# Dilated attention stage: paired loads and broadcasts merged, the combination's small operations moved to GpSimd, output-weight splits moved later

## The chip, the core and the metric

The kernel runs on one core of a Trainium2 chip. A core has a TensorE (PE in the profile) that multiplies matrices out of SBUF into PSUM banks, a VectorE (DVE), a ScalarE (ACT), a GpSimd (POOL) and a SyncE (SP), and 16 DMA engines that move data between DRAM and SBUF. The metric is the device time of one execution in microseconds, as the median of several runs. The time before is 1261.68 us (three runs, 1260.31 to 1263.06).

## The reference

One layer of an encoder over 1024 tokens of width 1024, in float32. A normed input is projected into two mixers. The first is a latent attention of 8 heads (MLA). The second, on which the change works, is a mixture of three dilated attentions: 24 heads of 64 columns in three groups of 8, group g with window and dilation (128, 1), (512, 4), (2048, 16). The three groups are joined for each head slot with weights from their softmax denominators.

```python
def dilated_group(q, k, v, dilation, side):
    ...
    s = jnp.where(valid, s, NEG_INF)
    m = jnp.max(s, axis=-1, keepdims=True)
    p = jnp.exp(s - m)
    den = jnp.sum(p, axis=-1)
    o = jnp.einsum('brhnqk,brhnkd->brhnqd', p.astype(v.dtype), vb).astype(jnp.float32) / den[..., None]
    lse = m[..., 0] + jnp.log(den)
    ...

def dilated_mixture(q, k, v, positions):
    ...
    for g, (window, dilation) in enumerate(DIL_CONFIGS):
        ...
        o, lse = dilated_group(q[:, :, sl], k[:, :, sl], v[:, :, sl], dilation, window // (2 * dilation))
        ...
    alpha = jax.nn.softmax(jnp.stack(lses, axis=0), axis=0)
    out = jnp.sum(alpha[..., None] * outs, axis=0)
    ...

def hybrid_layer(...):
    ...
    y_mla = (a_out * jax.nn.silu(z_mla)) @ w_o_mla
    y_dil = (d_out * jax.nn.silu(z_dil)) @ w_o_dil
    merged = sigmoid(g_mla + b) * y_mla + sigmoid(g_dil + b) * y_dil
    return x + merged @ w_out
```

The last lines are shortened: both branches are gated, projected, summed, and go through w_out; a last norm follows.

## The kernel before

**Numbers.** Matrix products in float32 are made of three products of a high and a low part (`mm3`, L142). `split` (L148) makes the parts: ScalarE casts the high one (L150), another engine subtracts for the low one (L151). Tensors for TensorE are kept as float32r; in DRAM many lie as pairs of high and low, which is the index p with two values.

**Stages.** Up to 541 us the kernel projects the input: latents, tables, values, then queries, keys and part of the gates, which it stores to DRAM. From 541 to about 840 us it runs the dilated stage, to about 1133 us the MLA attention with the output projections of both branches fed between its steps, and then the product with w_out (`output`). From the dilated stage on the order of all instructions is written by hand; nothing is rescheduled.

**The dilated stage.** `plan` (L1281) lists four pairs of heads with five items each: the two heads of group 0, the two of group 1 (`dil_head`, four units each) and one item for both heads of group 2 (`dil_classes`, two units). That makes 20 items and 72 units. `attention` (L1296) runs over the units: at step t it issues the transposes of unit t, the scores of unit t + 2, and so on, with projection matmuls fed between (`feed`). When the last unit of an item has been issued up to its scores, the query and key loads (`load_qk`) of the item two further on are issued, and two steps after the last unit its value load (`load_v`).

**Loads.** All DMAs are issued from SyncE by one line (L140), one after another, in the order of the code; a DMA whose semaphore isn't there yet holds all behind it. The buffers are rings of places in SBUF: queries (`op_b`, shown as at_2048), keys (`op_a`, shown as at_1152 or at_1024) and values (`op_c`) have two places each. A query tile of `dil_head` has 128 partitions with 2 x 1024 values: partitions 0 to 63 hold the 64 columns of the head in high and low part, and partitions 64 to 127 hold the same again, so it is loaded in two DMAs of 64 rows from the same source. The key tile has the high part in partitions 0 to 63 and the low part in 64 to 127, again two DMAs. `dil_classes` makes four loads of queries and four of keys, each of 64 rows, beside memsets of the zero parts.

**The combination.** After the last unit of a pair, `combine` (L1351) joins the three groups in steps that are put at fixed numbers of units later: statistics are transposed and stored to DRAM (s_sd), read back with 16 rows of 64 tokens each (`by_token`), weights are formed on VectorE with operations on 16x128 (`differences`, L1386 to 1390; `factors`, L1398 and 1401; `quotients`, L1405 to 1408), and are stored as six rows of 1024 (s_rr). `spread` (L1411) loads each row into 64 partitions, half a row at a time, 12 DMAs of 128 KB a pair, into the ring `bc` of five places. `weighted` (L1418) multiplies the three numerators by these on VectorE (L1421) and adds them on GpSimd (L1423), and the last sum is stored (s_da) except for the last pair. The first spreads are issued at step 5, the first products at step 7. For the last pair the steps lie in the MLA attention, by `LAST_STEPS` (L35).

**The w_out splits.** w_out is loaded in half-rows of 128x512 into `bc`, from step 112 of the MLA attention on (`wout_load`), and each is split two steps later (L1045): the cast on ScalarE, the subtraction on GpSimd. The last of the first eight is split in `output` (L1458), before `mla_sum`, `mla_weighted` and `mla_merged`.

The lines that the prediction's steps turn on:

```python
            for rows in (slice(0, 64), slice(64, 128)):
                self.dma(q[rows], self.dq[g][h].rearrange("c r p t -> (c r) p t"))
            for p in range(2):
                self.dma(k[64 * p:64 * p + 64, :S + pad], self.dk[g][h].rearrange("c r p t -> p (c r) t")[p])
...
                for h in range(2):
                    self.dma(r[64 * h:64 * h + 64], self.rr[pair, 2 * g + h, c].partition_broadcast(64))
```

Of the kernel before, what the change touches and what calls it, by code (L numbers as in the profile page):

```python
# [33 lines left out]
LAST_JOBS = [(dt, 0) for dt in range(4)] + [(dt + i, half) for dt in (4, 6) for half in range(2) for i in range(2)] + [(dt, 1) for dt in range(4)]  # L34
LAST_STEPS = {2: 4, 3: 6, 4: 8, 5: 10, 7: 14, 8: 16, 9: 18}  # L35
PIECES = (1, 0, 0), (3, 0, 1), (14, 3, 0), (16, 3, 1), (18, 1, 0), (20, 1, 1), (24, 2, 0), (26, 2, 1)
# [24 lines left out]
class Net:  # L61
# [455 lines left out]
    def block_steps(self, n, item, ps, tp):  # L517
# [45 lines left out]
        parts = 2 if g < 2 else 1  # L563
        dst = (self.dq if which == 0 else self.dk)[g][4 * quad:4 * quad + 4]
        off = 64 if (g == 0 and which) else 0
# [52 lines left out]
        def store(half):  # L618
            for i in range(2):
                for j in range(4):  # L620
                    x = slice(32 * j, 32 * j + 32)
                    if g < 2:
                        self.dma(dst[j, i, :, :, off + 512 * half:off + 512 * half + 512], st[i, half][x])
                    elif half:
                        self.dma(dst[j, i, :, 0], st[i, 0][x])

# [361 lines left out]
    def mla_attention(self, later, first):  # L988
# [29 lines left out]
        for t in range(128):  # L1018
# [41 lines left out]
    def dil_head(self, pair, g, hh, st, nums):  # L1060
# [116 lines left out]
    def dil_classes(self, pair, st, nums):  # L1177
# [6 lines left out]
        def load_qk():  # L1184
            q = o["q"] = self.get("op_b", [128, 2, 8, 2, 64])
            k = o["k"] = self.get("op_a", [128, 2, 8, 64])
            for hh in range(2):
                h = 2 * pair + hh
                for e in range(2):
                    r, c = slice(64 * e, 64 * e + 64), slice(512 * e, 512 * e + 512)  # L1190
                    nc.gpsimd.memset(q[r, hh, :, 1 - e], 0.0)
                    self.dma(q[r, hh, :, e], self.dq[2][h].rearrange("c r p t -> (c r) (p t)")[:, c].rearrange("r (b m) -> r b m", b=8))
                    self.dma(k[r, hh], self.dk[2][h].rearrange("c r p t -> (c r) (p t)")[:, c].rearrange("r (b m) -> r b m", b=8))

# [156 lines left out]
    def combine(self, pair, st, nums):  # L1351

        nc = self.nc
        v = nc.vector
# [29 lines left out]
        def differences():  # L1384
            w = o["w"] = self.get("c_w", [16, 4, 2, 64])
            v.tensor_copy(w[:, 3], nat(0, 0))  # L1386
            for g in (1, 2):
                v.tensor_tensor(out=wv(3, g), in0=wv(3, g), in1=nat(0, g), op=ALU.min)
            for g in range(3):
                v.tensor_tensor(out=wv(g, g), in0=wv(3, g), in1=nat(0, g), op=ALU.subtract)  # L1390

# [3 lines left out]
        def factors():  # L1395
            d = nat(1, 0)
            for g in range(3):
                v.tensor_tensor(out=nat(1, g), in0=wv(g, g), in1=nat(1, g), op=ALU.mult)  # L1398
            for g in (1, 2):
                y = d.rearrange("p h (m c) -> p h m c", c=DIL[g])  # L1400
                v.tensor_tensor(out=y, in0=y, in1=nat(1, g), op=ALU.add)

        def quotients():
            w, d = o["w"], nat(1, 0)
            v.tensor_scalar(out=d, in0=d, scalar1=2.0, scalar2=None, op0=ALU.mult)  # L1405
            v.reciprocal(out=d, in_=d)
            for g in range(3):
                v.tensor_tensor(out=w[:, g], in0=w[:, g], in1=d, op=ALU.mult)
            self.dma(self.rr[pair].rearrange("y (x t) -> x y t", t=64), w[:, 0:3].rearrange("p g h t -> p (g h) t"))

        def spread(half, gs):  # L1411
            c = slice(512 * half, 512 * half + 512)
            for g in gs:
                r = o[g, half] = self.get("bc")
                for h in range(2):
                    self.dma(r[64 * h:64 * h + 64], self.rr[pair, 2 * g + h, c].partition_broadcast(64))

        def weighted(half, gs):  # L1418
            c = slice(512 * half, 512 * half + 512)
            for g in gs:  # L1420
                v.tensor_tensor(out=nums[g][:, c], in0=nums[g][:, c], in1=o[g, half], op=ALU.mult)  # L1421
                if g:
                    nc.gpsimd.tensor_tensor(out=nums[0][:, c], in0=nums[0][:, c], in1=nums[g][:, c], op=ALU.add)  # L1423
            if half and 2 in gs and pair < 3:
                self.dma(self.da[pair], nums[0])
        return {-1: statistics, 0: by_token, 2: differences, 3: lambda: (exponents(), factors()), 4: quotients,
                5: lambda: (spread(0, range(3)), spread(1, (0, 1))),
                7: lambda: (weighted(0, (0, 1)), spread(1, (2,))), 8: lambda: (weighted(0, (2,)), weighted(1, (0,))), 9: lambda: weighted(1, (1, 2))}


    def output(self):
# [25 lines left out]
        self.mla_copied(31)  # L1457
        self.wout_split(0, nc.gpsimd)  # L1458
        self.mla_sum(31)
        self.mla_weighted(31)  # L1460
        self.mla_merged(31, v)
        for i in range(3):
            self.wout_load(i, 1)
        self.one_bank = False
        ready = []
        for n in range(16):
            while self.jobs_done <= 16 + n:
                next(self.fill)
            if n % 2 == 0:
                self.wout_split(1, nc.gpsimd)  # L1470
                if n < 10:
# [51 lines left out]
    def run(self):  # L1523
        tc, nc = self.tc, self.nc
        with ExitStack() as ctx:
# [5 lines left out]

            self.dq = [dt(f"s_dq{g}", (8, 2, 32, 2 if g < 2 else 1, S), F32R if g < 2 else F32) for g in range(3)]
            self.dk = [dt(f"s_dk{g}", (8, 2, 32, 2 if g < 2 else 1, S + (128 if g == 0 else 0)), F32R if g < 2 else F32) for g in range(3)]
            self.dv = [dt("s_dv0", (S + 128, 1024), F32R), dt("s_dv1", (S, 1024), F32R), dt("s_dv2", (S, 512))]
# [158 lines left out]
```

## Time and profile before

| quantity | value |
|---|---|
| time, median of three runs | 1261.68 us (1260.31 to 1263.06) |
| time of the profiled execution | 1265.36 us |
| its span, first to last instruction | 1263.5 us |
| mean granted TensorE clock | 0.992 |
| moved by DMA over the span | 212.99 MB in 131602 packets, 169 GB/s in the mean |
| DMA engines busy, mean | 58.1% of 16 engines' span |

The slices of the span (40 of 31.6 us; a digit is the busy share in tenths, PEclk the granted clock in tenths):

```profile
PE   8989999999999999999989899999899999989997
DVE  7483524567567652345575776748777767659442
ACT  6533437344434345456554555636665655654232
POOL 2352217887777777445363230411420111157222
PEclk9989999999999999999999999999999999999999
DMA  9947675266556643497878797856543254234241
```

The dilated stage lies in slices 18 to 26. The DMA row is at 7 to 9 tenths through most of them, the highest for so long a stretch. VectorE is at 5 to 7 there, ScalarE at about 5, GpSimd at 2 to 6. Engines run beside each other, so a busy share says nothing by itself of what ends last; the waits of TensorE do.

### The profile page before, as it was taken

To read this page: it belongs to the slowest core of one execution; us is meant where nothing else is said; L and a number is where in the kernel's file an instruction comes from. 1 tells how busy PE (TensorE), PEld (TensorE's weight loads), DVE (VectorE), ACT (ScalarE), POOL (GpSimd) and SP (SyncE) were. 2 spreads that over 40 slices of the span, in tenths; PEclk is the share of its full clock that TensorE was granted. 3 is DMA by queue.
4 is the path that set the end of the run, shared out by engine and by line. 5 is a ranking of instruction groups with operands and counts; after the bars stand their busy time and mean duration, and the time that the engine had idled before them with its cause. 6 is when DMAs were issued, how large, how long until landed. Compare 5 with 4: busy or idle time off the path is not lost.

```text
span 1263.5 us, 19551 instructions
## 1 busy us (share of the span) xinstructions
PE 1214.5 (96%) x6909; PEld 1063.2 (84%) x6909; DVE 764.2 (60%) x1373; ACT 621.0 (49%) x1300; POOL 535.5 (42%) x433
## 2 busy tenths in 40 slices
PE   8989999999999999999989899999899999989997
PEld 7979999788888888888878787978788888878886
DVE  7483524567567652345575776748777767659442
ACT  6533437344434345456554555636665655654232
POOL 2352217887777777445363230411420111157222
PEclk9989999999999999999999999999999999999999
DMA  9947675266556643497878797856543254234241
GB/s 325 274 152 264 224 283 159 84 177 167 138 135 158 169 125 117 129 260 205 207 207 211 186 259 191 240 156 165 154 140 105 81 126 125 93 101 167 84 150 50
DMA packets 131602, 212.99 MB, mean 169 GB/s; under 512 B 36841, under 2 KB 67121, under 8 KB 127601
## 3 DMA queue, kind: packets, MB, share of 16 engines
q1 hardware_dynamic: 131504, 211.75, 58.1%
q8 instruction: 54, 0.88, 0.3%
q14 instruction: 44, 0.35, 0.1%
HBM read 145.05 MB, written 66.65 MB: 168 GB/s over the span
## 4 chain that ended last, share of the span: by engine, by line
PE 72%; DMA 9%; DVE 8%; ACT 4%; issue 3%; POOL 2%; SPq 1%; ACTq 0%; DVEq 0%; POOLq 0%
PE bank L144 6%; PE bank L146 5%; PE bank L145 5%; PE bank L852 3%; PE st_a L144 2%; PE st_a L145 2%; PE st_a L146 2%; PE st_d L145 2%; PE st_c L145 2%; PE st_c L146 2%; PE st_d L146 2%; PE st_d L144 2%; PE st_c L144 2%; PE pj L144 2%; PE pj L145 2%
## 5 line engine op out<-in xcount | busy, mean ns | idle before, releaser
L151 POOL TENSOR_TENSOR w_l<-w_raw,w_h 128x512 fp32r<-128x512 f32 x188 | 246.7, 1326 | 300.1 <-ACT w_h L150 252.5
L150 ACT CAST w_h<-w_raw 128x512 fp32r<-128x512 f32 x188 | 112.4, 620 | 103.7 <-POOL w_raw L495 95.1
L144 PE MATMUL bank<-at_r,w_h 128*128 128x512 f32 x344 | 141.9, 412 | 5.6 <-DVE at_f L792 3.0
L860 DVE TENSOR_TENSOR at_r<-bank,at_r 128x512 fp32r<-128x512 f32 x128 | 87.9, 688 | 79.8 <-ACT at_r L854 79.5
L146 PE MATMUL bank<-at_r,w_l 128*128 128x512 f32 x344 | 135.3, 393 | 0.0
L145 PE MATMUL bank<-at_r,w_h 128*128 128x512 f32 x344 | 135.1, 393 | 0.0
L854 ACT CAST at_r<-bank 128x512 fp32r<-128x512 f32 x128 | 74.9, 585 | 81.0 <-PE bank L852 80.1
L144 PE MATMUL pj<-w_h,at_r 128*128 128x256 f32 x384 | 109.7, 286 | 0.0
L145 PE MATMUL pj<-w_l,at_r 128*128 128x256 f32 x384 | 109.4, 285 | 0.0
L146 PE MATMUL pj<-w_h,at_r 128*128 128x256 f32 x384 | 109.4, 285 | 0.0
L1116 ACT ACTIVATE at_f<-at_f,at_f 128x256 f32<-128x256 f32 x128 | 64.1, 501 | 70.8 <-DVE at_f L1109 70.7
L495 POOL TENSOR_TENSOR w_raw<-w_raw 128x512 f32<-128x512 f32 x64 | 83.7, 1308 | 0.0
L1135 DVE TENSOR_TENSOR at_r<-bank,at_r 128x512 fp32r<-128x512 f32 x64 | 44.0, 687 | 63.7 <-ACT at_r L1131 63.4
L852 PE MATMUL bank<-consts,at_f 128*128 128x128 f32 x512 | 77.0, 272 | 3.1 <-DVE at_r L860 2.0
L144 PEld LDWEIGHTS bank<-at_r,w_h 128*128 128x128 f32 x344 | 65.2, 190 | 16.8 <-DVE at_f L792 4.2
L146 PEld LDWEIGHTS bank<-at_r,w_l 128*128 128x128 f32 x344 | 64.8, 188 | 14.6
L144 PEld LDWEIGHTS pj<-w_h,at_r 128*128 128x128 f32 x384 | 74.2, 193 | 0.9
L145 PEld LDWEIGHTS pj<-w_l,at_r 128*128 128x128 f32 x384 | 74.1, 193 | 0.8
L146 PEld LDWEIGHTS pj<-w_h,at_r 128*128 128x128 f32 x384 | 74.1, 193 | 0.7
L145 PEld LDWEIGHTS bank<-at_r,w_h 128*128 128x128 f32 x344 | 65.3, 190 | 8.7
L876 PE MATMUL bank<-at_r,at_r 128*128 128x256 f32 x256 | 67.6, 285 | 1.9 <-ACT at_r L854 1.8
L877 PE MATMUL bank<-at_r,at_r 128*128 128x256 f32 x256 | 67.4, 285 | 1.8 <-DVE at_r L860 1.8
(320 smaller groups left out, 3331.1 us busy)
## 6 DMA issues: line engine op xcount, KB each, us to landing
w_raw<-wt SPq DMA_DIRECT2D x48, 512.0 KB, 4.4
at_r<-s_dq SPq DMA_DIRECT2D x32, 512.0 KB, 7.0
s_dq<-dq_st SPq DMA_DIRECT2D x80, 128.0 KB, 2.4
s_dk<-dq_st SPq DMA_DIRECT2D x80, 128.0 KB, 2.4
s_dv<-dv_st SPq DMA_DIRECT2D x32, 256.0 KB, 3.0
zt<-s_gt SPq DMA_DIRECT2D x32, 256.0 KB, 3.5
w_raw<-wv SPq DMA_DIRECT2D x12, 512.0 KB, 4.8
at_f<-s_rr SPq DMA_DIRECT2D x48, 128.0 KB, 3.2
```

The source lines that it names most:

```text
L144: mm(out, lh, rh, start=start, stop=False, skip_group_check=skip)
L145: mm(out, lh, rl, start=False, stop=False, skip_group_check=skip)
L146: return mm(out, ll, rh, start=False, stop=stop, skip_group_check=skip)
L150: self.nc.scalar.copy(out=h, in_=raw)
L151: sub.tensor_tensor(out=l, in0=raw, in1=h.bitcast(F32), op=ALU.subtract)
L495: self.nc.gpsimd.tensor_tensor(out=b[out], in0=b[x], in1=b[y], op=ALU.subtract)
L852: self.nc.tensor.transpose(pt[:, o:o + 128], self.P[k, b][:, 128 * kc:128 * kc + 128], self.ident)
L854: self.nc.scalar.copy(out=h, in_=pt)
L860: self.nc.vector.tensor_tensor(out=l, in0=pt, in1=h.bitcast(F32), op=ALU.subtract)
L876: mm(out, vv[:, kc], ph[:, x], start=kc == 0, stop=False)
L877: mm(out, vv[:, kc], pl[:, x], start=False, stop=kc == 7)
L1116: nc.scalar.activation(out=p, in_=p, func=AF.Exp, scale=-1.0, bias=nm, accum_out=den)
```

## The change

It has four parts.

1. **Merged transfers.** In `dil_head` the two query loads become one of 128 rows whose source is the same 64 rows twice (a leading dimension of 2 with stride 0), and the two key loads one of 128 rows whose source begins with the part p. In `spread` the two DMAs of 64 partitions become one of 128 rows from two rows of s_rr, each repeated 64 times (source 2 x 64 x length), and groups 0 and 1 are fetched for both halves at once, into two places of `bc` side by side. Instead of 12 spreads a pair there are four. In `dil_classes` queries come in two DMAs of 64x16x64 and keys in one of 128x1024; for that s_dq2 and s_dk2 lie in DRAM in another order, and the stores to them are cut as 32x2x512.
2. **Small operations.** 11 of the 16x128 operations of each pair go from VectorE to GpSimd, the doubling before the reciprocal becomes an addition of the tile to itself there, and a copy is dropped.
3. **Products.** Of the six products of numerators with spreads, the two of group 1 go to GpSimd, and the products and sums are put in another order over steps 7 to 10.
4. **w_out splits.** They start at step 116 in place of 114, and the last ones of the first half follow `mla_merged`; the first load of the second half is issued at step 127.

```diff
-LAST_STEPS = {2: 4, 3: 6, 4: 8, 5: 10, 7: 14, 8: 16, 9: 18}
+LAST_STEPS = {2: 4, 3: 6, 4: 8, 5: 10, 7: 13, 8: 15, 9: 17, 10: 19}
...
-                        self.dma(dst[j, i, :, 0], st[i, 0][x])
+                        self.dma(dst[2 * quad + j // 2, :, i, :, j % 2].rearrange("e r t -> r e t"), st[i, 0][x].rearrange("r (e t) -> r e t", e=2))
...
-            if t >= 114 and t % 2 == 0:
+            if t >= 116 and t % 2 == 0:
                 self.wout_split(0, nc.gpsimd)
+            if t == 127:
+                self.wout_load(0, 1)
...
-            for rows in (slice(0, 64), slice(64, 128)):
-                self.dma(q[rows], self.dq[g][h].rearrange("c r p t -> (c r) p t"))
-            for p in range(2):
-                self.dma(k[64 * p:64 * p + 64, :S + pad], self.dk[g][h].rearrange("c r p t -> p (c r) t")[p])
+            src = self.dq[g][h:h + 1].rearrange("h c r p t -> h (c r) (p t)")
+            self.dma(q.rearrange("p a t -> p (a t)"), src.to_broadcast([2, 64, 2 * S]))
+            self.dma(k[:, :S + pad], self.dk[g][h].rearrange("c r p t -> p (c r) t"))
...
+            for e in range(2):
+                r = slice(64 * e, 64 * e + 64)
+                nc.gpsimd.memset(q[r, :, :, 1 - e], 0.0)
+                self.dma(q[r, :, :, e].rearrange("r h b m -> r (h b) m"), self.dq[2][pair, e].rearrange("c r h (b m) -> (c r) (h b) m", m=64))
+            self.dma(k.rearrange("p h b m -> p (h b m)"), self.dk[2][pair].rearrange("e c r h t -> (e c r) (h t)"))
...
-            v.tensor_copy(w[:, 3], nat(0, 0))
...
-                v.tensor_tensor(out=wv(g, g), in0=wv(3, g), in1=nat(0, g), op=ALU.subtract)
+                p.tensor_tensor(out=wv(g, g), in0=wv(3, g), in1=nat(0, g), op=ALU.subtract)
...
-                v.tensor_tensor(out=nat(1, g), in0=wv(g, g), in1=nat(1, g), op=ALU.mult)
+                p.tensor_tensor(out=nat(1, g), in0=wv(g, g), in1=nat(1, g), op=ALU.mult)
...
-                v.tensor_tensor(out=y, in0=y, in1=nat(1, g), op=ALU.add)
+                p.tensor_tensor(out=y, in0=y, in1=nat(1, g), op=ALU.add)
+            p.tensor_tensor(out=d, in0=d, in1=d, op=ALU.add)
...
-            v.tensor_scalar(out=d, in0=d, scalar1=2.0, scalar2=None, op0=ALU.mult)
             v.reciprocal(out=d, in_=d)
...
-                v.tensor_tensor(out=w[:, g], in0=w[:, g], in1=d, op=ALU.mult)
+                p.tensor_tensor(out=w[:, g], in0=w[:, g], in1=d, op=ALU.mult)
...
+        def spread(g, first, c):
+            r = o[g, c.start] = self.shaped(self.places["bc"][0] + first, [128, c.stop - c.start])
+            src = self.rr[pair, 2 * g:2 * g + 2, c].rearrange("h (a t) -> h a t", a=1)
+            self.dma(r, src.to_broadcast([2, 64, c.stop - c.start]))
...
+        def spreads():
+            spread(1, 0, both)
+            spread(0, 4096, both)
+            spread(2, 8192, halves[0])
...
+        def step8():
+            weighted(0, 0, v)
+            add(1, 0)
+            weighted(2, 0, v)
+            add(2, 0)
...
+        def step9():
+            spread(2, 2048, halves[1])
+            weighted(0, 1, v)
+            add(1, 1)
...
+                5: spreads, 7: lambda: (weighted(1, 0, p), weighted(1, 1, p)), 8: step8, 9: step9, 10: step10}
...
-        self.wout_split(0, nc.gpsimd)
         self.mla_sum(31)
         self.mla_weighted(31)
         self.mla_merged(31, v)
-        for i in range(3):
+        self.wout_split(0, nc.gpsimd)
+        for i in range(1, 3):
```

TensorE executes the same instructions in the same order before and after. What moves stands on the other engines. In the rows below a name with at_ is a place in SBUF with its size in values (at_2048 a query tile, at_1152 a key or value tile, at_512 and at_1024 spreads, statistics or numerators), a name with s_ a tensor in DRAM, and xN the count of equal instructions in a row.

SyncE's queue, in the second pair of heads, from the store of the weights (s_rr) of the first pair to the store of its result (s_da). Before:

```order
L140 DMA s_rr<-at_512_f 16x6x64
L140 DMA at_512_f<-s_rr 64x512 x10
L140 DMA s_zs<-zt 128x512
L140 DMA at_1152_r<-s_dv_69 128x8x128
L140 DMA at_512_f<-s_rr 64x512 x2
L140 DMA at_2048_f<-s_dq_64 64x8x64
L140 DMA at_1024_f<-s_dk_67 64x512
L140 DMA at_2048_f<-s_dq_64 64x8x64
L140 DMA at_1024_f<-s_dk_67 64x512
```

And after, at the same place:

```order
L140 DMA s_rr<-at_512_f 16x6x64
L140 DMA at_1024_f<-s_rr 128x1x1024 x2
L140 DMA at_512_f<-s_rr 128x1x512
L140 DMA s_zs<-zt 128x512
L140 DMA at_1152_r<-s_dv_69 128x8x128
L140 DMA at_2048_f<-s_dq_64 64x16x64 x2
L140 DMA at_1024_f<-s_dk_67 128x1024
L140 DMA s_zs<-zt 128x512
L140 DMA at_512_f<-s_rr 128x1x512
L140 DMA w_raw<-wt 128x1024
L140 DMA s_da<-at_1024_f 128x1024
```

Twelve spreads have become four, of which the last stands behind the class loads, and eight class loads have become three; the store of s_da still ends the row, and the next pair's first loads stand behind it.

The same queue a little earlier in that pair, as one piece of the difference, with the loads of a head of group 1:

```order
 L140 DMA s_zs<-zt 128x512
 L140 DMA at_1152_r<-s_dv_69 128x8x128
-L140 DMA at_2048_r<-s_dq_63 64x2048 x2
-L140 DMA at_1152_r<-s_dk_66 64x1024 x2
+L140 DMA at_2048_r<-s_dq_63 128x1x2048
+L140 DMA at_1152_r<-s_dk_66 128x1x1024
 L140 DMA w_raw<-wt 128x1024
 L140 DMA s_rr<-at_512_f 16x6x64
```

Each of the two pairs of 64-row loads has become one of 128 rows, at the same place of the queue.

GpSimd's queue after, at the first combination; zt are gate values, w_l low parts of projection weights, at_768 the statistics by token. In the queue of before the gate operations and the subtractions w_l stand there alone:

```order
L1390 TENSOR_TENSOR at_512_f<-at_512_f,at_768_f 16x128 x3
L1398 TENSOR_TENSOR at_768_f<-at_512_f,at_768_f 16x128
L1398 TENSOR_TENSOR at_768_f<-at_512_f,at_768_f 16x2x16x4
L1398 TENSOR_TENSOR at_768_f<-at_512_f,at_768_f 16x2x4x16
L1401 TENSOR_TENSOR at_768_f<-at_768_f 16x128 x2
L1402 TENSOR_TENSOR at_768_f<-at_768_f 16x128
L1408 TENSOR_TENSOR at_512_f<-at_512_f,at_768_f 16x128 x3
L722 TENSOR_TENSOR zt<-zt 128x512
L723 TENSOR_TENSOR zt<-zt 128x512
L151 TENSOR_TENSOR w_l<-w_raw,w_h 128x512 x2
L1424 TENSOR_TENSOR at_1024_f<-at_1024_f 128x512 x2
```

Twelve small operations (the first seven rows) now stand ahead of the gate operations and of the products of group 1 (the last row).

More of the change, by code (lines that the diff above doesn't have):

```diff
@@ L563, in block_steps @@
         parts = 2 if g < 2 else 1
-        dst = (self.dq if which == 0 else self.dk)[g][4 * quad:4 * quad + 4]
+        dst = (self.dq if which == 0 else self.dk)[g]
+        dst = dst[4 * quad:4 * quad + 4] if g < 2 else dst
         off = 64 if (g == 0 and which) else 0
@@ L1186, in load_qk @@
             k = o["k"] = self.get("op_a", [128, 2, 8, 64])
[L1187 to L1193, printed above, removed]
+            for e in range(2):
[3 more added lines that the diff above has]
+            self.dma(k.rearrange("p h b m -> p (h b m)"), self.dk[2][pair].rearrange("e c r h t -> (e c r) (h t)"))
         def load_v():
@@ L1353, in combine @@
         nc = self.nc
-        v = nc.vector
+        v, p = nc.vector, nc.gpsimd
+        both, *halves = slice(0, S), slice(0, 512), slice(512, S)
         o = {}
@@ L1385, in differences @@
             w = o["w"] = self.get("c_w", [16, 4, 2, 64])
-            v.tensor_copy(w[:, 3], nat(0, 0))
-            for g in (1, 2):
-                v.tensor_tensor(out=wv(3, g), in0=wv(3, g), in1=nat(0, g), op=ALU.min)
+            v.tensor_tensor(out=wv(3, 1), in0=nat(0, 0).rearrange("p h (m c) -> p h m c", c=DIL[1]), in1=nat(0, 1), op=ALU.min)
+            v.tensor_tensor(out=wv(3, 2), in0=wv(3, 2), in1=nat(0, 2), op=ALU.min)
             for g in range(3):
-                v.tensor_tensor(out=wv(g, g), in0=wv(3, g), in1=nat(0, g), op=ALU.subtract)
+                p.tensor_tensor(out=wv(g, g), in0=wv(3, g), in1=nat(0, g), op=ALU.subtract)
         def exponents():
@@ L1403, in quotients @@
         def quotients():
             w, d = o["w"], nat(1, 0)
-            v.tensor_scalar(out=d, in0=d, scalar1=2.0, scalar2=None, op0=ALU.mult)
             v.reciprocal(out=d, in_=d)
             for g in range(3):
-                v.tensor_tensor(out=w[:, g], in0=w[:, g], in1=d, op=ALU.mult)
+                p.tensor_tensor(out=w[:, g], in0=w[:, g], in1=d, op=ALU.mult)
             self.dma(self.rr[pair].rearrange("y (x t) -> x y t", t=64), w[:, 0:3].rearrange("p g h t -> p (g h) t"))
[L1411 to L1424, printed above, removed]
+        def spread(g, first, c):
+            r = o[g, c.start] = self.shaped(self.places["bc"][0] + first, [128, c.stop - c.start])
+            src = self.rr[pair, 2 * g:2 * g + 2, c].rearrange("h (a t) -> h a t", a=1)
+            self.dma(r, src.to_broadcast([2, 64, c.stop - c.start]))
@@ new lines, in spreads, with weighted, add @@
+        def spreads():
+            spread(1, 0, both)
+            spread(0, 4096, both)
+            spread(2, 8192, halves[0])
+        def weighted(g, half, eng):
+            c = halves[half]
+            x = o[g, c.start] if g == 2 else o[g, 0][:, c]
+            eng.tensor_tensor(out=nums[g][:, c], in0=nums[g][:, c], in1=x, op=ALU.mult)
+        def add(g, half):
+            c = halves[half]
+            p.tensor_tensor(out=nums[0][:, c], in0=nums[0][:, c], in1=nums[g][:, c], op=ALU.add)
@@ L1425, in weighted, with step10 @@
+        def step8():
[3 more added lines that the diff above has]
+            add(2, 0)
+            self.turn["bc"] = 4
+        def step9():
+            spread(2, 2048, halves[1])
+            weighted(0, 1, v)
+            add(1, 1)
+        def step10():
+            weighted(2, 1, v)
+            add(2, 1)
+            if pair < 3:
                 self.dma(self.da[pair], nums[0])
         return {-1: statistics, 0: by_token, 2: differences, 3: lambda: (exponents(), factors()), 4: quotients,
-                5: lambda: (spread(0, range(3)), spread(1, (0, 1))),
@@ L1428, in combine @@
-                7: lambda: (weighted(0, (0, 1)), spread(1, (2,))), 8: lambda: (weighted(0, (2,)), weighted(1, (0,))), 9: lambda: weighted(1, (1, 2))}
+                5: spreads, 7: lambda: (weighted(1, 0, p), weighted(1, 1, p)), 8: step8, 9: step9, 10: step10}
     def output(self):
@@ L1468, in output @@
                 next(self.fill)
-            if n % 2 == 0:
-                self.wout_split(1, nc.gpsimd)
-                if n < 10:
+            if n % 2 == 0 or n == 1:
+                self.wout_split(n > 0, nc.gpsimd)
+                if n % 2 == 0 and n < 10:
                     self.wout_load(n // 2 + 3, 1)
@@ L1530, in run @@
             self.mv = dt("s_mv", (S, 1024), F32R)
-            self.dq = [dt(f"s_dq{g}", (8, 2, 32, 2 if g < 2 else 1, S), F32R if g < 2 else F32) for g in range(3)]
-            self.dk = [dt(f"s_dk{g}", (8, 2, 32, 2 if g < 2 else 1, S + (128 if g == 0 else 0)), F32R if g < 2 else F32) for g in range(3)]
+            by_class = (4, 2, 2, 32, 2, 512)
+            self.dq = [dt(f"s_dq{g}", (8, 2, 32, 2, S), F32R) for g in range(2)] + [dt("s_dq2", by_class)]
+            self.dk = [dt(f"s_dk{g}", (8, 2, 32, 2, S + (128 if g == 0 else 0)), F32R) for g in range(2)] + [dt("s_dk2", by_class)]
             self.dv = [dt("s_dv0", (S + 128, 1024), F32R), dt("s_dv1", (S, 1024), F32R), dt("s_dv2", (S, 512))]
```

## The prediction, made before the changed kernel ran

> **What bounds the kernel now.** I read the busy table and the slices first, then the stretch in which the change lies by windows and waits, then its transfers.
>
> ```profile
> PE 1214.5 (96%) x6909; PEld 1063.2 (84%) x6909; DVE 764.2 (60%) x1373; ACT 621.0 (49%) x1300; POOL 535.5 (42%) x433
> 600.00:620.00 20.00, 20.00 (x132) 18.03 (x130) 12.40 (x33) 11.90 (x33) 8.14 (x7) 1.00 0.81 208
> 660.00:680.00 20.00, 16.20 (x104) 14.26 (x105) 12.16 (x28) 9.99 (x25) 8.50 (x8) 1.00 1.03 255
> 700.00:720.00 20.00, 15.83 (x85) 12.65 (x84) 15.78 (x39) 8.59 (x24) 5.41 (x4) 0.93 0.65 170
> ```
>
> TensorE is busy for 96% of the span; it is the bound, and only its gaps can be won. The window rows (us, then PE, PEld, DVE, ACT, POOL, clock, DMA share, GB/s) show where: in the dilated stage a good window has PE at 20.00 of 20, a bad one at about 16, while the 16 DMA engines are busy for 0.65 to 1.03 of the time. The compared order has PE's instructions unchanged, so the change acts through PE's waits alone. The stage's ends and its waits (545 to 860 us):
>
> ```profile
> 525.40 1.14 SPq L140 DMA_DIRECT2D at_r<-s_dq  x2
> 543.13 0.36 PE L1099 MATMUL right<-at_r,at_r 128*128 128x256 f32 x1
> 835.80 0.94 DVE at_f L1248
> PE bank L1123 <- ACT at_f L1116: 9.2, 12, 2.7
> PE right L1099 <- DMA at_r<-s_dk: 3.0, 1, 3.0
> PE left L1147 <- DVE at_r L1135: 1.5, 1, 1.5
> PE bank L852 <- ACT at_f L844: 1.1, 1, 1.1
> PE left L144 <- DVE at_f L1248: 0.8, 1, 0.8
> PE left L1154 <- DVE at_r L1135: 0.3, 1, 0.3
> ```
>
> The first loads are issued at 525.4, the first scores run at 543, the last unit ends at 836.7: 294 us for 72 units, 4.1 us each. The waits sum to 15.9 us. That is all that an ideal edit of this stage could win.
>
> **The merged transfers.** These rows give what is merged (KB each):
>
> ```profile
> at_r<-s_dq SPq DMA_DIRECT2D x32, 512.0 KB, 7.0
> at_f<-s_rr SPq DMA_DIRECT2D x48, 128.0 KB, 3.2
> at_r<-s_dk SPq DMA_DIRECT2D x16, 288.0 KB, 9.2
> at_r<-s_dk SPq DMA_DIRECT2D x16, 256.0 KB, 8.8
> ```
>
> That is 16384 + 6144 + 4608 + 4096 = 31232 KB, or 32.0 MB, and merging leaves the bytes as they are. What changes is the outermost count of the source. Before, every such pattern began with 64 rows. After, q's source is [2][64][2048] (a repeat of 2 outside), k's is [2][64][1024 or 1152], and the spread's is [2][64][512 or 1024]; the destination has 128 rows. How many engines take part in a transfer can be read from windows that hold one transfer only:
>
> ```profile
> DMA packets 144, 0.26 MB, mean 87 GB/s; under 512 B 16, under 2 KB 16, under 8 KB 144
> q1 hardware_dynamic: 144, 0.26, 27.1%
> zt<-s_gt SPq DMA_DIRECT2D x1, 256.0 KB, 2.5
> DMA packets 16, 0.00 MB, mean 2 GB/s; under 512 B 8, under 2 KB 16, under 8 KB 16
> ```
>
> The first three rows (998 to 1001 us) are a load of 128 rows of 2 KB: 128 data packets and 16 small ones, one completion for each engine. The last (964.5 to 966.5 us) is the store of 8 rows of 512 B to s_mr: 8 data packets and 8 completions. So that store used 8 engines, though 8 more stood idle and its rows could have been halved. A transfer is cut between entries of the outermost count, not finer.
>
> No transfer of before has different outermost counts of which one is below 16, so the trace bounds the merged ones from both sides: 16 engines (if the destination's 128 rows decide) or 2 (if the source's 2 does). I take 2: the cut must fall between entries on both sides, and the source has two. By the Trainium skill ("DMA: Bandwidth & Descriptors", sections "Why a DMA increments its semaphore by 16 and not by 1" and "Rules for kernel authors") the count is the largest up to 16 that divides both outermost sizes, and a leading zero-stride broadcast of c copies confines a transfer to at most c engines. By that rule the sum is the one below, without it the first rival's; the 8 completions agree with it, and no run here shows a 2.
>
> The price is bytes by the rate of one engine:
>
> ```profile
> 505.00:510.00 5.00, 5.00 (x23) 4.14 (x23) 1.39 (x2) 1.60 (x3) 3.85 (x4) 1.00 0.32 130
> 555.00:558.00 3.00, 3.00 (x19) 2.64 (x19) 2.10 (x7) 1.91 (x6) 1.23 (x1) 1.00 1.00 225
> q1 hardware_dynamic: 57781, 64.30, 82.4%
> at_r<-s_dq SPq DMA_DIRECT2D x28, 512.0 KB, 7.0
> at_f<-s_rr SPq DMA_DIRECT2D x36, 128.0 KB, 3.1
> at_r<-s_dk SPq DMA_DIRECT2D x16, 256.0 KB, 8.8
> at_r<-s_dk SPq DMA_DIRECT2D x12, 288.0 KB, 9.2
> ```
>
> With few engines busy (first row, 128-row transfers), 130 / (0.32 x 16) = 25.4 GB/s an engine; with all of them on q and k (second row, 64-row halves), 225 / 16 = 14.1; the lone load above made 0.262 MB / (0.271 x 16 x 3 us) = 20.2. Two engines alone are nearest to the first: 25.4. The last pair's spreads (12 x 128 KB) fall behind the stage, so 30.4 MB is moved in it, 15.2 MB an engine: **599 us**, against 294 us in which the stage now runs.
>
> Those two engines also carry their sixteenth of everything else. From 541 to 841 us the 16 engines were busy for 0.824 x 16 x 300 = 3955 engine-us, of which the merged kinds (27.1 MB by the last four rows, at 14.1) took 1922; 2033 / 16 leaves **127 us** each.
>
> Do the two engines ever run dry? A load waits only for its buffer (two of each), which frees when the scores of the item before are issued; an item's four units take 16 us, its next load 31 (1.64 MB / 2 / 25.4), so mostly not. In two places of a pair they do, for SP issues in order. The spreads wait until the factors have landed, which queue behind k and q; then s_da's store, which waits for the last sum, stands ahead of the next pair's q. The first costs about 3 us, the second three units, 12 us: 15 a pair, **45 us** in the three pairs that have it. Small transfers queue behind large ones already now:
>
> ```profile
> at_f<-s_sd SPq DMA_DIRECT2D x12, 16.0 KB, 7.6
> s_rr<-at_f SPq DMA_DIRECT2D x4, 24.0 KB, 1.5
> ```
>
> 16 KB behind a q and a k takes 7.6 us, and 24 KB on emptier engines 1.5. After the last load about 10 us of units remain. The stage then ends at 525 + 599 + 127 + 45 + 10 = 1306 in place of 837: **+469 us**. In the attention behind it the last pair's 1.57 MB of spreads take 31 us on two engines, while VectorE reaches its first product some five ticks after their issue, waits there, and holds the low parts queued behind it that TensorE needs: about **+12 us**, an estimate.
>
> **The small operations.** Per pair 12 go to GpSimd and one copy goes away; two of six products follow, and the doubling becomes a sum.
>
> ```profile
> L1408 DVE TENSOR_TENSOR at_f<-at_f,at_f 16x128 f32<-16x128 f32 x9 | 5.8, 694 | 0.1
> L1390 DVE TENSOR_TENSOR at_f<-at_f,at_f 16x128 f32<-16x128 f32 x9 | 2.6, 338 | 0.1
> L1423 POOL TENSOR_TENSOR at_f<-at_f 128x512 f32<-128x512 f32 x12 | 16.4, 1368 | 33.8 <-DVE at_f L1421 30.0 <-DMA at_f<-s_rr 3.4
> ```
>
> GpSimd shows no operation on 16x128; on VectorE one takes 338 to 694 ns, and GpSimd's 128x512 takes 1368. So 12 cost between 4 and 16 us a pair in a chain that ends in a store. I take the lower half and put it at nothing: the transfers hide it. With that cover gone it would be up to 16 us a pair of later spreads, not of PE time, as the spreads have three units (12 us) before they are used. VectorE gains about 6 us a pair, off the path too.
>
> **The later splits.** ScalarE now stands 4.79 us on a load of w_out ahead of casts that TensorE needs:
>
> ```profile
> 1132.37 0.62 ACT L150 CAST at_r<-at_f 128x512 fp32r<-128x512 f32 x1 [4.79 <-DMA at_f<-w_out]
> PE bank L876 <- ACT at_r L854: 1.8, 1, 1.8
> ```
>
> TensorE waits 1.8 us of that. The split moves behind the last merge: **-2 us**, between 0 and -4.8.
>
> **Sum.** +469 + 12 - 2 = +479 us. The profiled execution took 1265.4 (span 1263.5 and 1.9 around it), 3.7 over the median of 1261.7; so about 1740 us.
>
> **Rivals.** (1) *All 16 engines take part*, the side of not slower: then 30.4 MB / 16 / 25.4 = 75 us an engine lies beside 294 of work, and of the 15.9 us of waits and the 1.8 at the splits about half goes: 1253; if the waits on ScalarE stay, 1262. The point is the number of engines: a pair has 73 us, 32 of them for other traffic, and 8.0 MB / n / 25.4 fits in the rest from n = 8 up. For it: 128 destination rows, and that 64-row halves run at 14.1. Against it: the 8 completions. The Trainium skill (the same page, "Rules for kernel authors") advises one 128-partition transfer in place of two halves; by that row alone this rival would come out, and no run shows it. (2) *Only a source without the repeat is cut in two* (k and spreads, not q): 13.6 MB / 2 / 25.4 = 268 us, with 127 and 45 over the stage's 294: about 1410. (3) *Two engines at the slow rate*: 15.2 / 14.1 = 1079 us, 2220.
>
> **Chances.** Two engines near 25.4: 0.82; rival 1 faster 0.07, same 0.04; rival 2 0.03; rival 3 0.04. Within the forecast, low: no dry places, half of the other traffic elsewhere, 1740 - 45 - 64 - 30 for a better rate = 1600. High: 20.2 GB/s gives 752 us for the 599: 1893, and some 20 us of restarts at a lower clock (0.93 in the bad window above): 1910. The range 1600 to 1910 holds about 0.8 of all; rivals stay outside. Slower by over 0.2% (what a measurement here tells from no change) 0.89, within 0.04, faster 0.07.
>
> **What would show it.** Right: q loads that land 40 us and more after issue, DMA share near 2/16 with some 50 GB/s through the stage, PE waiting on s_dq, s_dk or s_dv for most of its idle time, and two small packets for each merged transfer. Wrong: landings of 7 to 10 us, DMA share above 0.5 there, and PE's waits again on ScalarE and VectorE.

## The result and the profile after

The changed kernel took 1709.5 us (median of four runs, 1708.0 to 1714.9) against 1261.0 in the same comparison: a ratio of 1.356, 95% interval 1.3525 to 1.3597, or 448 us slower. The forecast was 1740, range 1600 to 1910.

First the page of the kernel after: two rows of busy time and transfers, and two of the 40 slices (of 42.8 us now).

```profile
PE 1270.4 (74%) x6909; PEld 1107.6 (65%) x6909; DVE 739.8 (43%) x1313; ACT 622.1 (36%) x1300; POOL 565.0 (33%) x481
PEclk9999999999998667787567677667697999999999
DMA  9666726646531223222222213231553544433521
q1 hardware_dynamic: 128976, 211.74, 40.0%
```

TensorE went from 96% busy to 74%, with the same 6909 matmuls. The bytes are the same, 211.7 MB, but the share of the 16 engines fell from 58.1% to 40.0% of a longer span: in slices 13 to 28, counted from 1, the DMA row stands at 1 to 3 tenths, where in the dilated stage it had been 7 to 9. TensorE waits, and so does most of the DMA. In that stretch the granted clock is also down to 5 to 8 tenths.

Windows (us, then PE, PEld, DVE, ACT, POOL, clock, DMA share, GB/s), the copies that end the units of group 2 (first and last start), and TensorE's waits from 545 to 1262 us:

```profile
561.00:1261.00 700.00, 334.94 (x1746) 289.73 (x1747) 167.98 (x435) 163.58 (x426) 131.11 (x133) 0.71 0.29 93
640.00:656.00 16.00, 14.41 (x82) 12.66 (x80) 6.51 (x22) 8.72 (x24) 5.72 (x5) 0.89 0.13 53
L1248 DVE COPY at_f<-left x8: 1004/1028/1053, 736.5 to 1262.3; 128x512 f32<-128x512 f32 x8
PE right L1101 <- DMA at_r<-s_dk: 209.6, 12, 24.3
PE left L1156 <- DVE at_r L1137: 74.2, 6, 22.6
PE bank L1125 <- ACT at_f L1118: 73.0, 5, 25.2
PE bank L146 <- POOL w_l L151: 29.3, 1, 29.3
```

The last of these copies started at 835.7 us before and starts at 1262.3 now: +427 us, nearly all of the loss, and in the stage itself, since its first loads are issued at 526.7 us in place of 525.4. From there to the end of the span it takes 450.5 us in place of 427.8. The wait on s_dk that came to 3.0 us in all is now 210, in 12 pieces of up to 24 us, and three more waits have grown behind it. The second row is the cause at a glance: when nothing but merged transfers is under way, the DMA share is 0.13, which is two of 16 engines, and they bring 53 GB/s.

### The profile page after: what moved, and what is told of

Read it like the earlier page. It is cut to its first block, busy times and chain, and to the rows that moved or that the text cites. A ratio compares the mean times of both kernels' runs of the same rounds, so it can differ in the third digit from the quotient of the medians.

```text
span 1712.8 us, 19408 instructions
## 1 busy us (share of the span) xinstructions
PE 1270.4 (74%) x6909; PEld 1107.6 (65%) x6909; DVE 739.8 (43%) x1313; ACT 622.1 (36%) x1300; POOL 565.0 (33%) x481
## 4 chain that ended last, share of the span: by engine, by line
DMA 30%; PE 27%; POOL 15%; SPq 10%; issue 8%; DVE 3%; ACT 2%; POOLq 0%; DVEq 0%; ACTq 0%
DMA at_r<-s_dk 11%; SPq L140 10%; POOL w_l L151 7%; DMA at_f<-s_rr 7%; POOL w_raw L495 5%; DMA s_rr<-at_f 4%; PE bank L144 3%; PE bank L146 3%; PE bank L145 3%; PE bank L853 3%; DMA s_zs<-zt 2%; DMA at_f<-s_sd 2%; PE bank L878 1%; PE left L146 1%; PE bank L877 1%
## 5 line engine op out<-in xcount | busy, mean ns | idle before, releaser
L1101 PE MATMUL right<-at_r,at_r 128*128 128x256 f32 x128 | 45.8, 373 | 209.6 <-DMA at_r<-s_dk 209.6
L146 PE MATMUL bank<-at_r,w_l 128*128 128x512 f32 x344 | 145.7, 424 | 29.3 <-POOL w_l L151 29.3
L1101 PEld LDWEIGHTS right<-at_r,at_r 128*128 128x128 f32 x128 | 29.6, 231 | 212.4 <-issue 192.9
L144 PE MATMUL bank<-at_r,w_h 128*128 128x512 f32 x344 | 154.0, 448 | 5.6 <-DVE at_f L793 3.0
L145 PE MATMUL bank<-at_r,w_h 128*128 128x512 f32 x344 | 146.3, 425 | 0.0
L1111 DVE CUSTOM_DVE_ANT_0 at_f<-right,masks 128x256 f32<-128x256 f32 x128 | 48.6, 417 | 168.2 <-PE right L1102 168.2
L1125 PE MATMUL bank<-consts,at_f 128*128 128x128 f32 x256 | 46.0, 303 | 73.2 <-ACT at_f L1118 73.0
L1125 PEld LDWEIGHTS bank<-consts,at_f 128*128 128x128 f32 x256 | 33.2, 155 | 80.4 <-ACT at_f L1118 78.2
L144 PEld LDWEIGHTS bank<-at_r,w_h 128*128 128x128 f32 x344 | 73.0, 212 | 18.7 <-DVE at_f L793 4.2
L878 PE MATMUL bank<-at_r,at_r 128*128 128x256 f32 x256 | 67.3, 285 | 21.9 <-DVE at_r L861 21.8
L1156 PE MATMUL left<-at_r,at_r 128*128 128x256 f32 x128 | 26.0, 326 | 74.2 <-DVE at_r L1137 74.2
```

The lines of the kernel that those rows point to most:

```text
L144: mm(out, lh, rh, start=start, stop=False, skip_group_check=skip)
L145: mm(out, lh, rl, start=False, stop=False, skip_group_check=skip)
L146: return mm(out, ll, rh, start=False, stop=stop, skip_group_check=skip)
L878: mm(out, vv[:, kc], pl[:, x], start=False, stop=kc == 7)
L1101: mm(s[:, c], q[:, 0, qs], kb, start=True, stop=False)
L1125: nc.tensor.transpose(pt[:, 128 * n:128 * n + 128], x["p"][:, 256 * i + 128 * c:256 * i + 128 * c + 128], self.ident)
```

## The experiments

**One transfer at a time.** Two kernels compute nothing of the layer. They load mostly 1 MB into 128 rows at a time and wait for each load; at the end come loads issued back to back, six of 2 x 64 rows and six of 128. In the first, the loads meant for its end ran beside the others, so it was made again with a fixed order:

```diff
...
+            def repeat(n):
+                m = 128 // n
+                one((r, x[0:m].rearrange("(a b) t -> a b t", a=1).to_broadcast([n, m, 2048])))
+            def strided(n):
+                one((r, x[0:128].rearrange("(b a) t -> a b t", a=n)))
...
```

> This kernel computes nothing of the layer and writes zeros: it loads 1 MB into 128 rows, one transfer at a time, and waits for each. Theory (a transfer is cut between the entries of its outermost count, so the count sets the engines): a source of 2 x 64 rows runs at 2 of 16 engines, share 0.12, some 53 GB/s, 20 us; 4 x 32 10 us; 8 x 16 5 us; 16 x 8 and 128 rows 3 to 5 us; the repeated and the strided forms alike at each count. Rows without a divisor suffer too: 124 rows (4 x 31) 10 us, 127 rows 39 us, 120 and 126 rows near 128. Spreads of 2 x 64 (0.5 MB) 10 us, as two 64-row transfers 2 to 3 us. Rival A (a repeat with stride 0 is slow because it reads the same rows again): repeats are slow at every count, strided ones of 2 x 64 as fast as 128 rows, and the two 64-row spreads are slow too. Rival B (one transfer of 1 MB is slow as such): 128 rows takes 20 us too. Six 2 x 64 loads issued back to back: if SyncE is held once a few large transfers are outstanding, the third or fourth issue takes about 20 us; otherwise all six are issued in some 4 us.

> The kernel of single transfers again, now with its order fixed, so that the six loads at its end no longer run beside the single ones (it computes nothing of the layer and writes zeros). From the undisturbed ones of the first time: 128 rows 5 us, two halves of 64 rows 5 to 7, 2 x 64 repeated 22, strided 22, 4 x 32 17 in both forms (53 GB/s by count alone would give 12, so something else than the count slows four engines: open), 8 x 16 12, 16 x 8 7, 124 rows 14, 127 rows 41, spread of 2 x 64 12, in two of 64 rows 5. Rival A (repeats are slow as such) would show the repeats slower than the strided ones at the same count. Six 2 x 64 loads back to back: SyncE held in the third or fourth issue for about 20 us if a queue is full after two, and not held otherwise; the six 128-row loads after them are issued in some 4 us.

Windows of the second kernel, each around one case: the window row (us, DVE, POOL, clock, DMA share, GB/s) of 128 plain rows, two halves, 2 x 64 repeated, and 4 x 32 repeated; then the packet rows of 2 x 64, 4 x 32, 8 x 16 and 16 x 8, and of 124, 126 and 127 plain rows.

```profile
3.00:8.00 5.00, 0.11 (x1) 0.00 (x0) 1.00 0.61 210
13.00:20.70 7.70, 0.25 (x3) 0.00 (x0) 1.00 0.61 136
21.00:43.50 22.50, 0.11 (x1) 0.00 (x0) 1.00 0.12 47
43.70:62.00 18.30, 0.00 (x0) 0.00 (x0) 1.00 0.21 57
DMA packets 130, 1.05 MB, mean 47 GB/s; under 512 B 2, under 2 KB 2, under 8 KB 2
DMA packets 132, 1.05 MB, mean 57 GB/s; under 512 B 4, under 2 KB 4, under 8 KB 4
DMA packets 136, 1.05 MB, mean 90 GB/s; under 512 B 8, under 2 KB 8, under 8 KB 8
DMA packets 144, 1.05 MB, mean 150 GB/s; under 512 B 16, under 2 KB 16, under 8 KB 16
DMA packets 128, 1.02 MB, mean 68 GB/s; under 512 B 4, under 2 KB 4, under 8 KB 4
DMA packets 140, 1.03 MB, mean 199 GB/s; under 512 B 14, under 2 KB 14, under 8 KB 14
DMA packets 128, 1.04 MB, mean 25 GB/s; under 512 B 1, under 2 KB 1, under 8 KB 1
```

The small packets are the completions, one for each engine that took part: 2, 4, 8, 16 for outermost counts of 2, 4, 8, 16, and 4, 14, 1 for 124, 126 and 127 rows, which are the largest numbers up to 16 that divide those rows. So the count sets the engines, as the Trainium skill states it ("DMA: Bandwidth & Descriptors", "Why a DMA increments its semaphore by 16 and not by 1"); before, this rested on one 8. The time until VectorE's copy could start, from its rows in the trace:

| source | us | | source | us |
|---|---|---|---|---|
| 128 rows | 4.9 | | 2 x 64, strided | 22.4 |
| 2 x 64 rows as two halves | 7.4 | | 4 x 32, strided | 18.0 |
| 2 x 64, repeated | 22.4 | | 8 x 16, strided | 11.6 |
| 4 x 32, repeated | 18.6 | | 16 x 8, strided | 7.4 |
| 8 x 16, repeated | 11.5 | | 124 / 126 / 127 rows | 15.1 / 5.2 / 41.3 |
| 16 x 8, repeated | 6.9 | | spread 2 x 64 (0.5 MB), merged / two | 12.6 / 4.9 |

Repeated and strided sources agree within 0.6 us at every count, so rereading the same rows is not the cause (rival A), and 128 plain rows are quickest, so size and merging are not either (rival B). The rate is not the count alone, though: with shares of 11.5% and 21.4%, unrounded, two engines moved 47 / (0.115 x 16) = 26 GB/s each, four 57 / (0.214 x 16) = 17. The form of the source has a part in it, since 124 plain rows, also on four engines and at a share of 20.3%, moved 68 / (0.203 x 16) = 21. Why it matters stays open.

**Undoing parts of the merging** in the changed kernel:

```diff
-            src = self.dq[g][h:h + 1].rearrange("h c r p t -> h (c r) (p t)")
-            self.dma(q.rearrange("p a t -> p (a t)"), src.to_broadcast([2, 64, 2 * S]))
-            self.dma(k[:, :S + pad], self.dk[g][h].rearrange("c r p t -> p (c r) t"))
+            for rows in (slice(0, 64), slice(64, 128)):
+                self.dma(q[rows], self.dq[g][h].rearrange("c r p t -> (c r) p t"))
+            for p in range(2):
+                self.dma(k[64 * p:64 * p + 64, :S + pad], self.dk[g][h].rearrange("c r p t -> p (c r) t")[p])
...
-            src = self.rr[pair, 2 * g:2 * g + 2, c].rearrange("h (a t) -> h a t", a=1)
-            self.dma(r, src.to_broadcast([2, 64, c.stop - c.start]))
+            for h in range(2):
+                self.dma(r[64 * h:64 * h + 64], self.rr[pair, 2 * g + h, c].partition_broadcast(64))
```

With both pieces undone, the queries and keys (first piece) and the spreads (second):

> The changed kernel with the queries, keys and spreads as transfers of 64 rows again; class loads, small operations, products and splits stay changed. Two-engine theory: all of the loss is gone, 1261 us within 6, and at best 1253. Rival (the small operations on GpSimd and the longer chain of the combination cost time of their own, which the transfers hide in the changed kernel): 1275 or more, with TensorE waiting behind GpSimd's low parts.

Measured: 1264.8, ratio 1.0029 (1.0012 to 1.0047). The loss is gone; all else that the change does costs at most half a per cent. With the first piece undone, so that only the spreads stay merged:

> Only the spreads (and class loads) stay merged. Two-engine theory: 4.7 MB of the stage on two engines take 89 us and do not fill them (with a sixteenth of all else some 280 of 294), but each pair's spreads land some 20 us late, hold the store of the sum and with it the next pair's loads: three stalls of 15 to 20 us and the last pair's 15, about 1325, between 1290 and 1380. Rival (only a repeat outside, that is the queries' form, is confined): 1261.

Measured: 1352.7 in one run, +91. The size is within the range, but the place is another than I expected: not the store of the sum and the loads behind it, but VectorE. Its waits, and TensorE's, in this kernel from 541 to 905 us:

```profile
DVE at_f L1425 <- DMA at_f<-s_rr: 80.5, 9, 18.6
PE left L1157 <- DVE at_r L1138: 63.2, 6, 21.2
```

VectorE stands at the first product (L1425) until the spread lands, and the low parts of the units (L1138) queue behind it; TensorE needs those. SyncE does stand 9.7 us at the first store of the sum too, from 666.1 to 675.8, but TensorE waits for queries or keys only 0.6 us in all. With the second piece undone, so that queries and keys stay merged:

> Queries and keys stay merged, spreads are 64-row transfers again. Two-engine theory: 25.7 MB at 53 GB/s are 485 us, with a sixteenth of the rest (some 104) and 20 of dry places the stage ends near 1145, about 1570 us in all, 140 less than the changed kernel, and the loss after the stage (26 us) shrinks. Rival (the spreads at the head of a pair's chain, with the held issues behind them, make most of the loss): under 1450.

Measured: 1616.4 in one run, +355. That is 46 over the expectation: I took off more for the spreads than they are worth (98 us by the profiled spans, 1712.8 against 1614.6). The two losses, 91 and 355, add up to 446 of the 448.

**The same transfer with other counts.** The keys alone were merged, and DRAM laid out so that the one DMA of 128 rows reads 2 x 64, 4 x 32 or 128 rows. The loads of the last two:

```diff
-            self.dma(k[:, :S + pad], self.dk[g][h].rearrange("c r p t -> p (c r) t"))
+            self.dma(k[:, :S + pad], self.dk[g][h].rearrange("r p c t -> (p c) r t"))
...
+            self.dma(k[:, :S + pad], self.dk[g][h].rearrange("p c r t -> (p c r) t"))
```

> Of the merged transfers only the keys of groups 0 and 1 (source 2 x 64 rows), the rest of the change as in the run with all split. Two-engine theory: 2.2 MB a pair at 53 GB/s are 42 us on two engines, and a sixteenth of the rest some 49, together 91 against the 73 that a pair has: about 1330, between 1290 and 1400. Rival (only large repeats hurt): 1261.

> The same keys with DRAM laid out so that the one transfer's source is 4 x 32 rows; nothing else differs. Theory (the outermost count sets the engines): 33 to 42 us x 2/4 to 1 of the load before, about 1285, between 1262 and 1320, clearly under the run with 2 x 64. Rival (a merged transfer of 128 rows is slow whatever its count): as with 2 x 64.

> The same keys with DRAM laid out so that the source is 128 rows in one run; still one transfer of 128 rows. Theory: 16 engines, the loss is gone, 1255 to 1266, and the DMA share of the stage falls under the 0.83 of before, since halves of 64 rows ran at 14 GB/s an engine and 128 rows at 25. Rival (merging itself, or one transfer in place of two, costs): over 1280.

Measured: 1373.7 and 1329.9, in one run each, and 1266.3 (ratio 1.0019, 0.9989 to 1.0049). The first window row below is of 2 x 64, the second of 4 x 32, the third of 128 rows, all from 541 to 835 us:

```profile
541.00:835.00 294.00, 219.11 (x1223) 190.81 (x1222) 121.39 (x314) 118.08 (x310) 104.67 (x103) 0.85 0.58 154
541.00:835.00 294.00, 243.72 (x1414) 213.20 (x1412) 134.15 (x354) 132.84 (x350) 108.40 (x106) 0.90 0.69 174
541.00:835.00 294.00, 281.32 (x1721) 247.31 (x1719) 168.55 (x429) 161.75 (x420) 133.18 (x133) 0.98 0.82 214
```

Same bytes, one transfer each, 128 destination rows each: the more engines, the more matmuls in the same 294 us. The case of 4 x 32 is 10 us over its range, in line with the 17 GB/s an engine above, by which four engines bring only some 1.3 times as much as two. The share of DMA fell to 0.82 only, not clearly under the 0.83 of before (0.84 with all split): for the keys the halves had cost little.

**Merged on 16 engines.** Keys as in the last case, and queries stored twice in DRAM, so that their load is 128 plain rows too:

```diff
+                            for copy in range(2):
+                                self.dma(dst[j, copy, i, :, :, c], st[i, half][x])
...
+            self.dma(q.rearrange("p a t -> p (a t)"), self.dq[g][h].rearrange("a c r p t -> (a c r) (p t)"))
```

> Queries and keys as single transfers of 128 rows on 16 engines: for the queries, s_dq of groups 0 and 1 holds every head twice, which costs 64 more stores of 128 KB (8.4 MB) in the stage before; spreads are 64-row transfers. Theory: the merge in itself neither costs nor pays much, 1255 to 1270; the stage keeps its 294 us. Alone, 128 rows took 4.9 us and two halves 7.4, so if the stage's waits hang on the loads it could gain up to 8 us (1253); if the extra stores push back the projections, 1275 and more, with the loss before 541 us.

Measured: 1255.5 (1253.5 to 1255.8), ratio 0.9945 (0.9927 to 0.9963): 0.5% faster than the kernel before. Its windows of the stage before and of the dilated stage, and the query loads in the latter (KB each, median us to landing):

```profile
200.00:541.00 341.00, 340.01 (x1593) 285.00 (x1592) 194.17 (x296) 146.87 (x283) 247.73 (x202) 1.00 0.59 172
541.00:835.00 294.00, 286.57 (x1766) 253.95 (x1765) 174.20 (x435) 168.98 (x432) 135.11 (x133) 0.98 0.70 216
at_r<-s_dq SPq DMA_DIRECT2D x14, 1024.0 KB, 6.0
```

The same 216 GB/s take 0.70 of the engines, not 0.83, and both copies of the queries land in 6.0 us where each half had taken 7.0. The stores that this costs do not show: they lie in the stage before, where the DMA share is 0.59 and TensorE busy for 340 of 341 us. The gain lies in the dilated stage: TensorE's waits from 541 to 850 us sum to 7.1 us, against 12.2 with all split and 15.9 before, and the last copy of group 2 starts at 823.3 us in place of 831.3 and 835.7. Keys alone brought no gain (1266.3); queries alone weren't tried.

**The other parts, each alone in the kernel of before.** The small operations, and the later splits:

```diff
...
-                v.tensor_tensor(out=nat(1, g), in0=wv(g, g), in1=nat(1, g), op=ALU.mult)
+                nc.gpsimd.tensor_tensor(out=nat(1, g), in0=wv(g, g), in1=nat(1, g), op=ALU.mult)
...
```

> The kernel before with the 12 small operations a pair on GpSimd alone. They took 0.39 to 0.56 us each there, 5.7 us a pair, in a chain whose last step has 12 us to spare: no difference, 1259 to 1265. Rival (GpSimd's low parts for TensorE are delayed behind them): 1267 or more.

Measured: 1260.0, ratio 0.9985 (0.9966 to 1.0004): no difference that can be told.

```diff
-            if t >= 114 and t % 2 == 0:
+            if t >= 116 and t % 2 == 0:
                 self.wout_split(0, nc.gpsimd)
+            if t == 127:
+                self.wout_load(0, 1)
...
-        self.wout_split(0, nc.gpsimd)
         self.mla_sum(31)
         self.mla_weighted(31)
         self.mla_merged(31, v)
-        for i in range(3):
+        self.wout_split(0, nc.gpsimd)
+        for i in range(1, 3):
...
```

> The kernel before with the later splits of w_out alone. The wait of 4.8 us of ScalarE, of which TensorE waited for 1.8, goes: -2 us, 1257 to 1262. Rival (the wait is replaced by one on the next load or behind the merges): no difference or slower.

Measured: 1263.0, ratio 1.000 (0.9981 to 1.0018). Waits from 1100 to 1250 us, the first row of the kernel before (TensorE waits there for no low part of GpSimd) and the last two of this one:

```profile
ACT at_r L150 <- DMA at_f<-w_out: 6.6, 3, 4.8
```

```profile
ACT at_r L150 <- DMA at_f<-w_out: 1.2, 3, 0.7
PE left L146 <- POOL w_l L151: 2.8, 1, 2.8
```

ScalarE's wait on w_out did go, and with it TensorE's 1.8 us behind it. In its place TensorE waits 2.8 us for the low part of a projection weight (w_l), which on GpSimd now queues behind splits of w_out; the same wait stands in the changed kernel and in the run with all split. The interval is 2.3 us wide to either side, so the time alone can't tell -2 from 0; these waits speak for the rival.

## Why the prediction was right, step by step

- **The bound and the place** (gaps of TensorE, in the dilated stage): right; 427 of the 449 us between the two profiled spans lie there.
- **Two engines, since the source's count decides**: right, and shown by the completions and by the series of 2, 4 and 128. Rival 1 (16 engines) and rival 2 (only the repeat is spared or cut) are out: 2 x 64 strided takes as long as repeated, and spreads alone cost 91 us. Rival 3 (two engines at 14.1 GB/s each) is out by the next step. One sign came in part only: the share near 2/16 with 50 GB/s showed where merged transfers ran alone, while the stage's mean was 0.29 and 93 GB/s.
- **599 us for 30.4 MB**: the 2 x 64 loads issued back to back land every 19.8 us (the first four), which is 1.05 MB at 53.0 GB/s or 26.5 an engine in place of 25.4: 574 us.
- **127 us for the rest of the traffic**: from 527 to 1262 us the engines were busy for 0.29 x 16 x 735 = 3410 engine-us; less 2 x 574 leaves 2262, a sixteenth of which is 141. As in the prediction this spreads the rest evenly.
- **45 us in dry places and 10 at the end**: oversized, as 574 + 141 leaves only 20 of these 735. The 45 were 3 us a pair ahead of the spreads and 12 at the store of the sum. SyncE did stand at that store for 10 to 11 us in each of the three pairs: the rows below show no issue from 856.7 to 866.6 us, and the next pair's queries 1.9 us behind the store. But for most of that time the two engines still carried the last spread, issued at 855.4 (share 0.13, 50 GB/s from 862 to 864). They stood dry for some 2 us only: the share was 0.00 from 865.5 to 867.0 (last row), and in the next two pairs from 1047.1 to 1049.1 and from 1229.4 to 1232.0. What the prediction had not priced inside the stage is that spreads hold VectorE and the low parts behind it, as the run with spreads alone shows. Together the three terms are 43 under the forecast of 1306 for the stage's end (1263).

```profile
856.04 0.68 SPq L140 DMA_DIRECT2D w_raw<-wt  x1
866.59 0.32 SPq L140 DMA_DIRECT2D s_da<-at_f  x1
868.51 0.94 SPq L140 DMA_DIRECT2D at_r<-s_dq  x1
865.50:867.00 1.50, 1.19 (x4) 0.90 (x4) 0.94 (x5) 0.87 (x3) 1.50 (x2) 0.51 0.00 0
```

- **+12 us behind the stage**: 23, and the step had the mechanism right. In the attention VectorE stands 19.7 us before its first product of the last pair (first row below), TensorE 21.2 behind it. With spreads alone merged the stretch from the last copy to the end is 451 us (1350.9 less 900.0), with queries and keys alone 429 (1614.6 less 1185.3), so these 23 are the spreads'. The second fence has the copies of these two kernels.

```profile
1320.42 0.69 DVE L1424 TENSOR_TENSOR at_f<-at_f 128x512 f32<-128x512 f32 x1 [19.71 <-DMA at_f<-s_rr]
PE bank L878 <- DVE at_r L861: 21.8, 2, 21.2
```

```profile
L1249 DVE COPY at_f<-left x8: 1008/1034/1062, 606.0 to 900.0; 128x512 f32<-128x512 f32 x8
L1248 DVE COPY at_f<-left x8: 1005/1030/1057, 731.7 to 1185.3; 128x512 f32<-128x512 f32 x8
```

- **Small operations, nothing**: right, and not only under the cover of the transfers, since alone in the kernel before they cost nothing that can be told. The lower half of 4 to 16 us a pair holds too: GpSimd's groups of them in the run with all split sum to 22.7 us, 5.7 a pair:

```profile
L1399 POOL TENSOR_TENSOR at_f<-at_f,at_f 16x128 f32<-16x128 f32 x12 | 5.7, 500 | 4.7 <-ACT at_f L1394 4.7
L1391 POOL TENSOR_TENSOR at_f<-at_f,at_f 16x128 f32<-16x128 f32 x12 | 5.7, 492 | 41.8 <-DVE at_f L1389 41.8
L1409 POOL TENSOR_TENSOR at_f<-at_f,at_f 16x128 f32<-16x128 f32 x12 | 5.2, 451 | 4.2 <-DVE at_f L1407 4.2
L1402 POOL TENSOR_TENSOR at_f<-at_f 16x128 f32<-16x128 f32 x8 | 4.5, 559 | 0.3
L1403 POOL TENSOR_TENSOR at_f<-at_f 16x128 f32<-16x128 f32 x4 | 1.6, 390 | 0.3
```

- **Later splits, -2 us**: the step "the split moves behind the last merge: -2 us" had its mechanism wrong, though its range of 0 to -4.8 holds what was measured (0, with 2.3 us to either side). The wait goes as it says, but the splits now delay a low part of GpSimd's that TensorE needs, and a wait of 2.8 us stands in place of the 1.8.
- **The sum**: 1740 against 1709.5, in part by luck. The stage came out 43 us shorter than forecast, the stretch behind it about 11 longer, and the splits gave 2 less; these make up the 31 us of difference. Within the stage, too, the rest of the traffic was forecast 14 too low and the other two terms 25 and 35 too high.

What stays open: with queries, keys and spreads in 64-row transfers again 0.29% (0.12 to 0.47) is left, though small operations and splits cost nothing alone. Whether the reordered products, the class loads or the longer spreads bring it wasn't tried.

## What to carry to other kernels

Before two DMAs are merged, look at the outermost count of both patterns as they will be after the merge: in these runs, all with a destination of 128 rows or of as many as the source, the number of engines was the largest up to 16 that divides the source's outermost count, and a leading dimension of 2 (two copies, two parts, two heads) turned a 16-engine transfer into one on two engines. A destination with a smaller outermost count than the source's wasn't tried. If the merge is wanted, change the layout in DRAM until the source is plain rows, even at the price of storing a tensor twice. And price a moved wait by what will then be last on every engine that the moved instructions queue on: the splits gave up 1.8 us in one queue and lost 2.8 in another.

## What had not been expected

**SyncE is held by large transfers on few engines.** In the kernel of single loads, of six 2 x 64 loads issued back to back the first two issues take 0.6 and 0.5 us and the third 19.7, about the time of one load; so it looks as if no more than some two of these can be outstanding. The row below has the second and third issue together:

```profile
252.32 20.31 SPq L63 DMA_DIRECT2D more<-x  x2
```

In the changed kernel this hits transfers that use all engines. Some of SyncE's rows (start, us of the issue), a GpSimd row, and a TensorE row, with what they waited for:

```profile
545.12 13.62 SPq L140 DMA_DIRECT2D at_r<-s_dq  x1
558.87 6.46 SPq L140 DMA_DIRECT2D s_gt<-dq_st  x3
567.89 13.73 SPq L140 DMA_DIRECT2D at_r<-s_dv  x1
581.72 11.40 SPq L140 DMA_DIRECT2D s_gt<-dq_st  x1
598.70 0.09 POOL L1262 MEMSET area<- 1x1 f32 x1 [64.09 <-DMA s_gt<-dq_st]
600.91 0.79 PE L146 MATMUL bank<-at_r,w_l 128*128 128x512 f32 x1 [29.28 <-POOL w_l L151]
```

A store of s_gt stands in the queue behind the held loads until 593 us, GpSimd waits 64 us for it, and TensorE 29 us for GpSimd. How much of the 448 us this adds to what two engines cost anyway wasn't separated.

**The clock falls with the waits.** In the stage the granted clock was 0.71 in the mean, and 0.50 while TensorE stood still:

```profile
545.00:560.00 15.00, 0.00 (x0) 0.00 (x0) 0.00 (x0) 0.00 (x0) 0.00 (x0) 0.50 0.26 84
```

Much the same matmuls took 335 us of the stage in place of 280. How much of that lengthens the stalls and how much hides behind the transfers wasn't separated.

**Plain rows beat 16 x 8 rows.** Both use 16 engines, and 1 MB takes 4.9 us in the one form and 6.9 to 7.4 in the other; two halves of 64 rows side by side take 7.4. No run here says why.
